# A hybrid encoder trunk: rounded value rows and sums of squares, sums given out a head pair later

## The chip, the cores and the metric

The kernel runs on one core of a Trainium2 chip, in one launch. The metric is the device time of the launch in microseconds (us), as the median of three runs. Beside it there is the trace of one profiled execution. Of the core's engines five matter here: TensorE (PE in the trace; PEld are its weight loads), VectorE (DVE), ScalarE (ACT), GpSimd (POOL) and SyncE (SP, on whose queue all DMAs are issued). Each works through its own list of instructions in order and waits for others through semaphores.

## The reference

The trunk has two layers over 16 learned tokens and 512 others, 1024 features wide. A layer is a token mixer of two parallel branches and then a gated FFN. One branch is a gated delta rule with 8 heads (GDN, solved in both directions), the other a retention with 4 heads. The output drops the learned tokens.

```python
def token_mixer(h, w_in, conv_w, ...):
    proj = h @ w_in
    (qkv_a, z_a, a_in, b_in, q_b, k_b, v_b, g_b, gate_a, gate_b) = jnp.split(proj, ...)
    qa, ka, va = jnp.split(short_conv(qkv_a, conv_w), ...)        # then l2norm of qa, ka
    g = -jnp.exp(a_log) * softplus(a_in + dt_bias);  beta = sigmoid(b_in)
    o_a = gated_delta(qa, ka, va, g, beta) forward + the same backward
    y_a = (rms(o_a) * gdn_gain * silu(z_a)) @ w_up_a
    o_b = rms(retention(qr, kr, vr) forward + backward)           # sum over m of gamma^|n-m| (q_n.k_m) v_m
    y_b = (o_b * silu(g_b)) @ w_up_b
    merged = sigmoid(gate_a) * y_a + sigmoid(gate_b) * y_b
    return merged @ w_out
for i in range(2):
    h = h + token_mixer(rms_norm(h, norm_mix[i]), ...)
    h = h + swiglu(rms_norm(h, norm_ffn[i]), ...)
return rms_norm(h, norm_final)[:, 16:]
```

`rms` needs, per token and head, a sum of squares over the head's value channels: 128 for a GDN head, 512 for a retention head.

## The kernel before, in words

Activations lie feature by token: 128 partitions of features, 528 columns of tokens (16 learned, then 4 blocks of 128). Layer 0 goes through them in two halves of 264 columns (`FULL`); layer 1, whose learned tokens are not in the output, mostly in 512 (`TAIL`).

**Projections.** A weight block of 1024 x 128 is loaded (`weights`, L183), and `split` (L177) makes two tiles in a rounded f32 type of it: the high part on ScalarE, the rest by a subtraction on VectorE. Activations are split in the same way (xh, xl). `mm3` (L193) then multiplies high by high, high by rest and rest by high: three matmuls per 128 features. Every matmul is issued by `mm`, L112, so that in the trace one tells them apart by their tiles: mmps is a projection, rpv the retention's value product, oms a sum of squares, rs the retention's scores, kvt and kvm turns of tokens, lvy, yy, oo, ks and their like the steps of a GDN head.

**The GDN heads** come in four pairs. `gdn_begin` projects the pair's q, k and v, convolves them and turns them into token rows; with the first pair `scalars` (L435) projects the 32 decay columns and turns them. `gdn_chain` then makes the products (L538), the decayed copies (L600), solves the 32-token diagonal blocks with small DMAs (L613), joins them in two levels (L629), and scans the blocks forward and backward (L723). In the levels the block matrix N is the sum of two tiles (GpSimd), small blocks are expanded to block-diagonal tiles by a product with a mask (`spread`: QT, QT2, TT on VectorE, Qf and Qb on GpSimd), and the matmuls lvy take QT, N and TT, the scan takes Qf and Qb. At the end `gdn_out` (L807) squares the head's output and its q on ScalarE, combines them on VectorE and calls `mean_square` (L790), where a plain f32 matmul with a column of ones sums over partitions. ScalarE takes the sum out of PSUM and a DMA stores it.

**Retention** (L878) has per head: two projections with rotation, scores rs with a decay strip (VectorE) and a split into prh and prl; then per 128 value channels a projection, a turn to token rows (rv, split), a gate projection, and the value product rpv: for each of the four token blocks three rounded matmuls on 128 rows, and for the 16 learned tokens one plain f32 matmul on 16 rows (prm, rvm). Squares are added up on VectorE, and `mean_square` sums them at the head's end.

**What sets the order.** `weave` (L985) runs a pair's chain and a filler side by side and gives out so much filler for so much chain; the filler is the retention heads 0 to 2 and the gates z and merge, and `retention(3)` follows the last pair. The scheduler of the framework then orders the instructions of each engine by priority and by a timeline of its own, within what buffers allow. PSUM has three pools of one bank per tile: mmps (2 buffers), the retention's and the norms' small tiles (`pt`, 2 buffers in rotation), the GDN chain's tiles (`ct`, 4 buffers). The SBUF tag "gcr" has four buffers: the pair's four broadcast decay rows, which a DMA fills from `grow`.

The work is single-file on SP: loads of weight blocks (wraw) and the small loads and stores of the chains stand in one queue in the order that the scheduler gives them.

## Time and profile before

| what | value |
|---|---|
| runs | 2978.34, 2980.01, 2978.48 us; median 2978.48 |
| profiled execution | 2975.5 us, span of the trace 2973.7 us |
| mean granted TensorE clock | 0.991 of full speed |
| TensorE | busy 2873.8 us (97%), 19519 matmuls |
| VectorE, ScalarE, GpSimd | busy 1781.4 (60%), 1038.8 (35%), 64.1 us (2%) |
| chain that ended last, by engine | TensorE 83%, VectorE 7%, DMA 6%, ScalarE 2% |

A row of the timeline gives the start (us from the span's start), the busy time of the group, the engine, the source line, the operation, output<-inputs by the program's names, partitions x elements and type, the count, and in brackets the idle time before it with what ended that. Records of matmuls overlap and their ends are modelled, so that what a matmul costs is read from one start to a later one. A plain f32 matmul leaves two records where a rounded one leaves one.

### The profile page before, as it was taken

How to read it: one execution, taken by the hardware profiler on the slowest of the kernel's cores; microseconds unless marked ns; L12 is line 12 of the kernel's file. 1: busy time of each engine (PE TensorE's matmuls, PEld its weight loads, DVE VectorE, ACT ScalarE, POOL GpSimd, SP SyncE). 2: the span in 40 equal slices, each digit the busy share in tenths (PEclk: the TensorE clock that was granted, in tenths of full speed). 3: DMA queues.
4: the chain of work that ended last, by engine and by line, in shares of the span. 5: the costliest groups of instructions: out<-in, count | busy, mean ns of one | idle time of the engine just before them, and what ended most of it. 6: DMA issues, size and time to landing. Idle time of an engine off the chain costs nothing.

```text
span 2973.7 us, 48710 instructions
## 1 busy us (share of the span) xinstructions
PE 2873.8 (97%) x19519; PEld 2578.0 (87%) x19519; DVE 1781.4 (60%) x3769; ACT 1038.8 (35%) x1967; POOL 64.1 (2%) x156
## 2 busy tenths in 40 slices
PE   8999999999999999999999999999999999999998
PEld 8998998889989998999998787887878878888887
DVE  6867867768456445333358769587685474534333
ACT  4434334244333233222244243343333332322222
POOL 0000000000000000000000000000000000000000
PEclk9999999999999999999999999999999999999999
DMA  4422323323337342333344323233234284433333
GB/s 138 111 74 75 105 75 100 84 74 107 90 106 228 118 141 81 91 93 100 115 115 115 83 76 100 71 93 97 66 101 109 74 260 126 135 99 92 98 101 99
DMA packets 506420, 313.46 MB, mean 105 GB/s; under 512 B 55632, under 2 KB 460778, under 8 KB 506194
## 3 DMA queue, kind: packets, MB, share of 16 engines
q1 hardware_dynamic: 506194, 310.35, 36.4%
q8 instruction: 153, 2.51, 0.3%
q14 instruction: 73, 0.60, 0.1%
HBM read 265.28 MB, written 45.01 MB: 104 GB/s over the span
## 4 chain that ended last, share of the span: by engine, by line
PE 83%; DVE 7%; DMA 6%; ACT 2%; issue 1%; SPq 0%; DVEq 0%; ACTq 0%
PE mmps L112 66%; PE rpv L112 3%; PE rs L112 2%; PE oo L112 2%; PE fu L112 2%; DVE wlo L118 1%; PE sn L112 1%; DMA xd<-w 1%; PE yy L112 1%; DMA gcr<-grow 1%; PE ks L112 1%; DMA lo<-od_b 1%; ACT whi L178 1%; PE oms L112 1%; PE lvy L112 1%
## 5 line engine op out<-in xcount | busy, mean ns | idle before, releaser
L112 PE MATMUL mmps<-xh,whi 128*128 128x264 f32 (+2 forms) x3888 | 1213.8, 312 | 22.8 <-ACT rp L894 9.3
L112 PE MATMUL mmps<-xh,wlo 128*128 128x264 f32 (+2 forms) x3888 | 1204.5, 310 | 1.1 <-DVE wlo L118 1.1
L112 PE MATMUL mmps<-xl,whi 128*128 128x264 f32 (+2 forms) x3888 | 1202.3, 309 | 0.0
L112 PEld LDWEIGHTS mmps<-xh,whi 128*128 128x128 f32 x3888 | 737.6, 190 | 77.6 <-issue 13.3
L112 PEld LDWEIGHTS mmps<-xh,wlo 128*128 128x128 f32 x3888 | 736.3, 189 | 44.3 <-issue 9.1
L112 PEld LDWEIGHTS mmps<-xl,whi 128*128 128x128 f32 x3888 | 736.6, 189 | 39.5 <-issue 5.9
L118 DVE TENSOR_TENSOR wlo<-wraw,whi 128x1024 fp32r<-128x1024 f32 (+1 forms) x394 | 477.3, 1212 | 486.5 <-ACT whi L178 482.0
L178 ACT CAST whi<-wraw 128x1024 fp32r<-128x1024 f32 (+1 forms) x394 | 410.0, 1041 | 936.5 <-PE mmps L112 723.7
L112 PE MATMUL mmps<-oh,whi 128*128 128x264 f32 (+2 forms) x1126 | 359.2, 320 | 3.7 <-DVE mrg L115 3.7
L112 PE MATMUL mmps<-ol,whi 128*128 128x264 f32 (+2 forms) x1126 | 358.6, 319 | 0.0
L112 PE MATMUL mmps<-oh,wlo 128*128 128x264 f32 (+2 forms) x1126 | 357.9, 318 | 0.0
L112 PEld LDWEIGHTS mmps<-oh,whi 128*128 128x128 f32 x1126 | 211.7, 188 | 21.6 <-ACT oh L178 3.4
L112 PEld LDWEIGHTS mmps<-ol,whi 128*128 128x128 f32 x1126 | 211.7, 188 | 16.5 <-issue 1.3
L112 PEld LDWEIGHTS mmps<-oh,wlo 128*128 128x128 f32 x1126 | 211.9, 188 | 15.6
L115 DVE SCALAR_TENSOR_TENSOR ac<-xc,cw,ac 128x528 f32<-128x528 f32 x192 | 146.7, 764 | 8.1 <-ACT ac L125 1.7
L118 DVE TENSOR_TENSOR ff<-fg,mmps 128x264 f32<-128x264 f32 (+1 forms) x63 | 32.5, 516 | 116.8 <-PE mmps L112 116.8
L112 PE MATMUL rpv<-prh,rv 128*128 128x264 f32 (+1 forms) x384 | 98.4, 328 | 0.0
L118 DVE TENSOR_TENSOR st<-w 68x30 f32<-68x30 f32 (+14 forms) x240 | 78.3, 326 | 28.1 <-DMA w<-ndm 16.4
L125 ACT ACTIVATE gth<-mmps 128x264 f32<-128x264 f32 (+1 forms) x135 | 61.3, 454 | 68.3 <-PE mmps L112 67.9
L118 DVE TENSOR_TENSOR w<-w,st 68x30 f32<-68x30 f32 (+14 forms) x240 | 78.0, 325 | 6.0
L112 PE MATMUL rs<-rot 128*128 128x264 f32 (+3 forms) x240 | 77.9, 456 | 0.7 <-DVE pr L118 0.7
L112 PEld LDWEIGHTS rpv<-prh,rv 128*128 128x128 f32 x384 | 65.3, 188 | 10.5 <-issue 6.0
(298 smaller groups left out, 3064.6 us busy)
## 6 DMA issues: line engine op xcount, KB each, us to landing
wraw<-in_w_in_dram SPq DMA_DIRECT2D x194, 512.0 KB
wraw<-in_w_ffn_in_dram SPq DMA_DIRECT2D x88, 512.0 KB
wraw<-in_w_up_b_dram SPq DMA_DIRECT2D x32, 512.0 KB
wraw<-in_w_ffn_out_dram SPq DMA_DIRECT2D x32, 512.0 KB
gcr<-grow SPq DMA_DIRECT2D x32, 264.0 KB
wraw<-in_w_up_a_dram SPq DMA_DIRECT2D x16, 512.0 KB
wraw<-in_w_out_dram SPq DMA_DIRECT2D x16, 512.0 KB
wraw<-in_w_ffn_out_dram SPq DMA_DIRECT2D x16, 384.0 KB
```

Source lines behind the costliest of these rows:

```text
L112: newest[0] = nc.tensor.matmul(o, lhsT=l, rhs=r, start=start, stop=stop)
L115: (eng or nc.vector).scalar_tensor_tensor(out=o, in0=a, scalar=s, in1=b, op0=op0, op1=op1)
L118: (eng or nc.vector).tensor_tensor(out=o, in0=a, in1=b, op=op)
L125: nc.scalar.activation(o, a, f, **kw)
L178: nc.scalar.copy(hi, src)
```

## The change

Five things are changed.

1. The value product's learned tokens: scores and values of the 16 learned tokens are split too and laid under one another in tiles of 96 rows (pst: high, rest, high; vst: high, high, rest; 16 rows used of each 32), so that one rounded matmul sums the three products.
2. The sums of squares: the summed tile is split (osh, osl for GDN heads; prh, prl for retention heads), and two rounded matmuls with a rounded column of ones take the place of one f32 matmul.
3. A pair's or head's sums are put on a list (`later`) and issued afterwards by `sums`: in the next pair's `gdn_begin` after its second head's front and at its end, in the next retention head behind its rotation, and at the end of the mixing. The square of a GDN head's q moves from `gdn_out` to the decayed copies. osh and osl take buffers of the tag "gcr".
4. The decay columns: high part and rest of the 32 columns' weights lie side by side in one tile, so that two matmuls per 128 features do; the two halves of the result are added after the turns, which are 64 columns wide.
5. In the levels N is added on VectorE, and Qf and Qb are expanded on ScalarE, four activations each, with the mask's column as the scale.

```diff
+    one = cp.tile([P, 1], F32R, name="one")
+    nc.scalar.copy(one, ones[:, 0:1])
...
     def scalars():
+
         ab = gp.tile([P, L], F32, name="ab", tag="gcr", bufs=4)
-
-        def consume(t, n0, n, ps):
-            nc.vector.tensor_copy(ab[0:32, n0:n0 + n], ps[0:32])
-        project(W, C_AB, 1, xn, FULL, consume)
+        with tc.high_priority(offset=lead[0]):
+            raw = wp.tile([P, 8, P], F32, name="wraw", tag="wraw", bufs=WB[0])
+            nc.sync.dma_start(raw, W[:, C_AB:C_AB + P].rearrange("(k p) c -> p k c", p=P))
+            w = wp.tile([P, 8, P], F32R, name="whi", tag="whi", bufs=WB[1])
+            nc.scalar.copy(w, raw)
+            tt(w[:, :, 32:64], raw[:, :, 0:32], w[:, :, 0:32].bitcast(F32), SUB)
+        for n0, n in FULL:
+            ps = pmm.tile([P, 512], F32, name="mmps", tag="mm")
+            for k in range(KT):
+                for j, t in enumerate(xn):
+                    mm(ps[:, :n], w[:, k, :], t[k][:, n0:n0 + n], start=k + j == 0, stop=k + j == KT)
+            nc.vector.tensor_copy(ab[0:64, n0:n0 + n], ps[0:64, :n])
         ps = ct("abt")
         for c in range(NC):
-            nc.tensor.transpose(ps[:, c * 32:(c + 1) * 32], ab[0:32, NM + c * P:NM + (c + 1) * P], ident[:32, :32])
-        nc.tensor.transpose(ps[0:NM, P:P + 32], ab[0:32, 0:NM], ident[:32, :32])
+            nc.tensor.transpose(ps[:, c * 64:(c + 1) * 64], ab[0:64, NM + c * P:NM + (c + 1) * P], ident[:64, :64])
+        nc.tensor.transpose(ps[0:NM, 256:320], ab[0:64, 0:NM], ident[:64, :64])
         abt = gp.tile([P, NCH, 2, 16], F32, name="abt", tag="sc", bufs=SB)
         nc.vector.memset(abt[:, NC], 0.0)
-        nc.vector.tensor_copy(abt[:, 0:NC].rearrange("p c s h -> p (c s h)"), ps[:, 0:P])
-        nc.vector.tensor_copy(abt[0:NM, NC].rearrange("p s h -> p (s h)"), ps[0:NM, P:P + 32])
+        for n, c0, c1 in ((P, 0, NC), (NM, NC, NCH)):
+            o = abt[0:n, c0:c1].rearrange("p c s h -> p c (s h)")
+            a = ps[0:n, c0 * 64:c1 * 64].rearrange("p (c j e) -> p c j e", j=2, e=32)
+            nc.vector.tensor_copy(o, a[:, :, 0])
+            tt(o, o, a[:, :, 1], ADD)
...
@@ -604,6 +618,7 @@
             gr = s["gr"][d]
             act(gr, gr, AF.Exp)
             tt(gr, gr, s["q"], MUL)
+        act(s["q"][:, t0:L], s["q"][:, t0:L], AF.Square)
         for c in range(NCH):
             n = tok(c)[1]
...
@@ -634,7 +649,7 @@
         xd = st["xd"]
         nn, nb = s["N"]
         fl = lambda a: a.rearrange("p c d -> p (c d)")
-        tt(fl(nn), fl(nn), fl(nb), ADD, eng=nc.gpsimd)
+        tt(fl(nn), fl(nn), fl(nb), ADD)
...
-        def spread(o, a, m, n, eng=None):
+        def spread(o, a, m, n):
             tt(o.rearrange("p c (b i) -> p c b i", b=n), bc(a.unsqueeze(2), [P, NC, n, 32]),
-               bc(m.unsqueeze(1).unsqueeze(3), [P, NC, n, 32]), MUL, eng=eng)
+               bc(m.unsqueeze(1).unsqueeze(3), [P, NC, n, 32]), MUL)
...
         T, Q, Qf, Qb = (gp.tile([P, NC, P], F32, name=n, tag="NQ", bufs=8) for n in ("QT", "QT2", "Qf", "Qb"))
         TT = gp.tile([P, NC, 64], F32, name="TT", tag="sc", bufs=SB)
         spread(T, tm, cst["bm"], 4)
         spread(Q, qm, cst["bm"], 4)
         spread(TT, tl, cst["bm2"], 2)
-        spread(Qf, qf, cst["bm"], 4, nc.gpsimd)
-        spread(Qb, qb, cst["bm"], 4, nc.gpsimd)
+        for o, a in ((Qf, qf), (Qb, qb)):
+            for b in range(4):
+                act(o[:, :, b * 32:b * 32 + 32], a, AF.Copy, scale=cst["bm"][:, b:b + 1])
...
@@ -792,7 +808,8 @@
         ms = ms[0:1]
         for n0, n in tail:
             ps = pt("oms")
-            mm(ps[0:1, :n], ones[:, 0:1], sq[:, n0:n0 + n])
+            for j in range(2):
+                mm(ps[0:1, :n], one, sq[j][:, n0:n0 + n], start=j == 0, stop=j == 1)
             act(ms[:, n0:n0 + n], ps[0:1, :n], AF.Copy, scale=scale, bias=bias)
         nc.sync.dma_start(msd[row:row + 1, :], ms[:, t0:L])
...
-    def gdn_out(h, st):
+    def gdn_squares(h, st):
+
         s = st[h]
         (o, om), q = s["o"], s["q"]
         o = o.rearrange("p c d -> p (c d)")
@@ -814,11 +832,18 @@
         if not last:
             nc.sync.dma_start(od_a[h, :, 0:NM], om)
             act(sq[:, 0:NM], om, AF.Square)
-        act(q[:, t0:L], q[:, t0:L], AF.Square)
         stt(sq[:, t0:L], q[:, t0:L], 128.0 * 128.0 * EPS, sq[:, t0:L], MUL, ADD)
+        hi, lo = (gp.tile([P, L], F32R, name=n, tag="gcr", bufs=4) for n in ("osh", "osl"))
+        split(hi[:, t0:L], lo[:, t0:L], sq[:, t0:L])
+        later.append(lambda ps: mean_square(h, (hi, lo), 4.0 / 128.0, 4 * 128 * EPS * 4 * EPS, tmp("ms"), ps))
         yield 1.0
-        mean_square(h, sq, 4.0 / 128.0, 4 * 128 * EPS * 4 * EPS, s["gr"][0], ct)
-        yield 1.0
+
+    later = []
+
+    def sums(ps):
+
+        while later:
+            later.pop(0)(ps)
...
+                if h == hs[1]:
+                    sums(ct)
                 lead[0] = PRI
...
         for _ in sc:
             pass
+        sums(ct)
...
-        for pair in zip(*[gdn_out(h, st) for h in hs]):
-            yield sum(pair)
+        for h in hs:
+            yield from gdn_squares(h, st)
+
+
+
+    pst = rp.tile([96, L], F32R, name="pst")
+    vsts = [rp.tile([96, P], F32R, name=f"vst{q}") for q in range(2)]
+    for t in (pst, *vsts):
+        nc.gpsimd.memset(t.bitcast(F32), 0.0)
...
         q, k = rot
+        sums(pt)
         yield from filler
         pr = []
         for c in range(NCH):
             m0, m = tok(c)
-            o = tmp("pr") if c < NC else rp.tile([P, L], F32, name="prm", tag="prm")
+            o = tmp("pr")
...
                 pr.append((hi, lo))
             else:
-                pr.append(o)
+                split(pst[0:NM, t0:L], pst[32:32 + NM, t0:L], o[0:NM, t0:L])
+                nc.scalar.copy(pst[64:64 + NM, t0:L], pst[0:NM, t0:L].bitcast(F32))
             yield 1.8
...
             rv = rp.tile([P, 2, NC * P], F32R, name="rv", tag="rot", bufs=2)
             vh, vl = rv[:, 0], rv[:, 1]
-            vm = rp.tile([NM, P], F32, name="rvm", tag="rvm", bufs=2)
+            vst = vsts[dv % 2]
             ps = pt("rvt")
             for c in range(NC):
                 n0, n = tok(c)
@@ -942,7 +979,8 @@
             split(vh, vl, ps)
             pm = pt("rvm")
             nc.tensor.transpose(pm[0:NM, 0:P], vc[:, 0:NM], ident)
-            nc.scalar.copy(vm, pm[0:NM, 0:P])
+            split(vst[0:NM], vst[64:64 + NM], pm[0:NM, 0:P])
+            nc.scalar.copy(vst[32:32 + NM], vst[0:NM].bitcast(F32))
             gs = tmp("rg")
...
                 for c in range(NC):
                     for a, b in ((vh, 0), (vh, 1), (vl, 0)):
                         mm(ps[:, :n], a[:, c * P:(c + 1) * P], pr[c][b][:, n0:n0 + n], start=c + b == 0 and a is vh, stop=False)
-                mm(ps[:, :n], vm, pr[NC][0:NM, n0:n0 + n], start=False)
+                mm(ps[:, :n], vst, pst[:, n0:n0 + n], start=False)
...
             nc.sync.dma_start(od_b[h * 4 + dv, :, t0:L], o[:, t0:L])
             if dv:
                 tt(sqa[:, t0:L], sqa[:, t0:L], sq[:, t0:L], ADD)
             yield 4.5
-        mean_square(H + h, sqa, 4.0 / DV, 4 * 256 * EPS, tmp("ms"), pt)
+        sq = [rp.tile([P, L], F32R, name=n, tag=n, bufs=4) for n in ("prh", "prl")]
+        split(sq[0][:, t0:L], sq[1][:, t0:L], sqa[:, t0:L])
+        later.append(lambda ps: mean_square(H + h, sq, 4.0 / DV, 4 * 256 * EPS, tmp("ms"), ps))
...
     for _ in retention(3, merge_gates(14, 16)):
         pass
+    sums(pt)
     mixctx.close()
```

The framework's scheduler orders the result anew. Two places show it, both on TensorE in layer 1. The first is the end of a pair's scan, between the third and the fourth pair. yy and oo are the scan's last matmuls, oms the sums of squares, kvt and kvm the turns of the next pair's tokens, mmps projections. Before:

```order
L112 MATMUL yy<-r,Qf 128x128 x2
L112 MATMUL oo<-gcr,S 128x128 x2
L112 MATMUL oo<-P,xx 128x128 x2
L112 MATMUL oms<-qk,c_ones 1x512 x2
L525 MATMUL kvt<-c_ident,qk 128x128 x4
L526 MATMUL kvm<-c_ident,qk 16x128
L526 MATMUL kvm<-c_ident,v_23772 16x128
L525 MATMUL kvt<-c_ident,v_23772 128x128 x4
L112 MATMUL mmps<-xh,whi 128x264
```

The same place of the changed kernel:

```order
L112 MATMUL yy<-r,Qf 128x128 x2
L112 MATMUL oo<-gcr,S 128x128 x2
L112 MATMUL oo<-P,xx 128x128
L539 MATMUL kvt<-c_ident,qk 128x128 x4
L112 MATMUL oo<-P,xx 128x128
L540 MATMUL kvm<-c_ident,qk 16x128
L540 MATMUL kvm<-c_ident,v_24000 16x128
L539 MATMUL kvt<-c_ident,v_24000 128x128 x4
L112 MATMUL mmps<-xh,whi 128x264
```

The sums are gone from between the scan and the turns. They stand 24 projection matmuls later, one at a time, the last of the four 19 projection matmuls behind the first. At layer 0's pair ends the order is the same in kind, with the first sums about 35 projection matmuls behind the turns.

The second place is the last pair of layer 1, at the end of its scan. rpv are the value products of the fourth retention head, rs its scores. Before, the scan's matmuls stand among that head's:

```order
L112 MATMUL rpv<-prh,rv 128x512
L112 MATMUL oo<-P,xx 128x128
L112 MATMUL rpv<-prh,rv 128x512
L112 MATMUL oo<-P,xx 128x128
L112 MATMUL rpv<-prl,rv 128x512
L112 MATMUL rpv<-prh,rv 128x512 x2
```

In the changed kernel:

```order
L112 MATMUL ks<-S,qk 128x128 x2
L112 MATMUL yy<-r,Qf 128x128 x2
L112 MATMUL oo<-gcr,S 128x128 x2
L112 MATMUL oo<-P,xx 128x128 x2
L112 MATMUL oms<-osh,one 1x512 x2
L112 MATMUL oms<-osl,one 1x512 x2
L112 MATMUL rs<-rot 128x512 x4
L112 MATMUL mmps<-xh,whi 128x264
```

Before, that head's projections, scores and value products lay between the scan's steps, and the pair's two sums came between projections (`mmps<-xl,whi`, `oms<-qk,c_ones` x2, `mmps<-xh,wlo`). Now the head's q and k projections stand earlier, the scan's steps follow one another, and the sums stand straight behind the scan and ahead of the head's scores. At the end of layer 0's last pair the order is the same: eight oo, eight oms, then rs.

## Rows read from the trace of the kernel before

**Rows 1.** The page: busy time of each engine (share of the span) xinstructions.
```profile
PE 2873.8 (97%) x19519; PEld 2578.0 (87%) x19519; DVE 1781.4 (60%) x3769; ACT 1038.8 (35%) x1967; POOL 64.1 (2%) x156
```
**Rows 2.** Waits of TensorE: waiting tile <- releaser; us in all, count, the longest.
```profile
PE lvy L112 <- DVE QT L118: 13.8, 8, 4.9
```
**Rows 3.** Chain that ended last, in order of time: start, us, engine, tile, xcount.
```profile
40.01 22.73 PE mmps L112 x186
...
2609.49 249.62 PE mmps L112 x1078
```
**Rows 4.** Timeline of TensorE, a value product in layer 0: start, busy, instruction.
```profile
297.04 0.29 PE L112 MATMUL rpv<-prh,rv 128*128 128x264 f32 x1
297.26 0.71 PE L112 MATMUL rpv<-prm,rvm 16*128 16x264 f32 x2
...
298.13 0.28 PE L112 MATMUL rpv<-prl,rv 128*128 128x264 f32 x1
```
**Rows 5.** The same timeline, a value product in layer 1.
```profile
1861.14 0.40 PE L112 MATMUL rpv<-prh,rv 128*128 128x512 f32 x1
1861.47 1.12 PE L112 MATMUL rpv<-prm,rvm 16*128 16x512 f32 x2
...
1862.75 0.28 PE L112 MATMUL mmps<-xl,whi 128*128 128x264 f32 x1
```
**Rows 6.** The same, a retention head's two sums in layer 0.
```profile
304.16 0.28 PE L112 MATMUL mmps<-xh,wlo 128*128 128x264 f32 x1
304.38 1.05 PE L112 MATMUL oms<-rsq,c_ones 128*1 128x264 f32 x4
...
305.58 0.28 PE L112 MATMUL mmps<-xl,whi 128*128 128x264 f32 x1
```
**Rows 7.** The same, the end of a pair in layer 0; idle time before in brackets.
```profile
451.10 0.39 PE L112 MATMUL oo<-Pm,xx 16*128 16x16 f32 x2
452.04 1.05 PE L112 MATMUL oms<-qk,c_ones 128*1 128x264 f32 x4 [0.55 <-DVE qk L115]
...
457.30 0.39 PE L112 MATMUL mmps<-xh,whi 128*128 128x264 f32 x1 [0.45 <-ACT xc L507]
```
**Rows 8.** Groups by form: operation xcount | busy us, mean ns | idle before, releaser.
```profile
L178 ACT CAST prh<-pr 128x528 fp32r<-128x528 f32 x16 | 10.2, 635 | 33.5 <-DVE pr L118 30.6 <-DVE Nm L567 2.8
L118 DVE TENSOR_TENSOR prl<-pr,prh 128x528 fp32r<-128x528 f32 x16 | 11.3, 703 | 3.2 <-ACT prh L178 3.1
```
**Rows 9.** Timeline of TensorE and ScalarE, the end of a pair in layer 1.
```profile
2136.13 0.49 PE L112 MATMUL yy<-r,Qf 128*128 128x128 f32 x2 [1.18 <-DVE r L115]
2136.90 0.65 PE L112 MATMUL oo<-P,xx 128*128 128x128 f32 x4
2137.78 1.15 ACT L125 ACTIVATE qk<-o 128x512 f32<-128x512 f32 x2
2139.19 3.43 PE L112 MATMUL oms<-qk,c_ones 128*1 128x512 f32 x4 [1.64 <-DVE qk L115]
...
2144.91 0.39 PE L112 MATMUL mmps<-xh,whi 128*128 128x264 f32 x1 [0.96 <-ACT xc L507]
```
**Rows 10.** Window, length, busy (xcount) of PE, PEld, DVE, ACT, POOL; PEclk, DMA, GB/s.
```profile
2140.00:2150.00 10.00, 9.04 (x55) 6.34 (x53) 5.41 (x10) 4.68 (x9) 0.13 (x2) 0.86 0.29 56
```
**Rows 11.** Timeline of GpSimd, VectorE and TensorE in the levels, layer 1.
```profile
1700.55 1.04 POOL L118 TENSOR_TENSOR Qb<-qe,c_bm 128x512 f32<-128x512 f32 x1 [5.08 <-DVE qe L651]
1700.94 0.93 DVE L118 TENSOR_TENSOR TT<-qe,c_bm 128x256 f32<-128x256 f32 x1
1701.79 1.28 DVE L118 TENSOR_TENSOR QT<-qd,c_bm 128x512 f32<-128x512 f32 x2
1702.61 2.05 PE L112 MATMUL lvy<-QT,N 128*128 128x128 f32 x8 [4.01 <-DVE QT L118]
```
**Rows 12.** Timeline of the queue of SyncE, layer 0: start, us of the group, issue.
```profile
266.74 1.15 SPq L554 DMA_DIRECT2D gcr<-grow  x2
275.96 21.91 SPq L187 DMA_DIRECT2D wraw<-in_w_in_dram  x4
```

More of the change, by code (lines that the diff above doesn't have):

```diff
@@ L382, in layer @@
 def layer(tc, nc, env, l, xn, gd):
-    (x, meta, newest, lead, cp, dp, wp, xp, tp, mm, stt, tt, ts, act, tmp, ctmp, pt, ct, pmm, cst, ident, ones, cw, gain,
+    (x, meta, newest, lead, cp, dp, wp, xp, tp, mm, stt, tt, ts, act, tmp, ctmp, pt, ct, pmm, cst, ident, ones, one, cw, gain,
      prm, softplus, inverse_root, nea, lg, lgn, hd, split, weights, mm3, FULL, TAIL, Norm, xtiles,
@@ L386, in layer @@
         "x", "meta", "newest", "lead", "cp", "dp", "wp", "xp", "tp", "mm", "stt", "tt", "ts", "act", "tmp", "ctmp", "pt", "ct", "pmm",
-        "cst", "ident", "ones", "cw", "gain", "prm", "softplus", "inverse_root", "nea", "lg", "lgn",
+        "cst", "ident", "ones", "one", "cw", "gain", "prm", "softplus", "inverse_root", "nea", "lg", "lgn",
         "hd", "split", "weights", "mm3", "FULL", "TAIL", "Norm", "xtiles", "first_units",
```

## Prediction

> **What bounds the kernel now.** I read the engines' busy shares first. TensorE is busy 97% of the span, VectorE 60%, ScalarE 35%, GpSimd 2% [rows 1]. The reader is to see that an instruction taken off VectorE, ScalarE or GpSimd is worth nothing by itself. What counts is TensorE's own time and the few places where TensorE stands still. Second, the waits: the longest of those that the change touches is TensorE's for a block table in the levels, 13.8 us in all [rows 2]. Third, the chain that ended last. It is TensorE for 83%, in stretches that hold nothing but projection matmuls, and these give the price of one pass of the rounded type: 22.73/186 = 0.122 us for 264 columns in layer 0, 249.62/1078 = 0.232 us for 512 columns in layer 1 [rows 3]. Last, TensorE's timeline at the lines that the diff touches. Records there overlap, so a cost is read from start to start, less the passes between.
>
> **The change, part by part**, against the profiled execution (2975.5 us; its span is 2973.7).
>
> A. *Learned tokens' value rows.* In layer 0 a 16-row f32 matmul stands between rounded ones. From the start of the one before it to the start of the second one behind it are 298.13 - 297.04 = 1.09 us; without the two passes of 0.122 it takes 0.846 [rows 4]. In layer 1 the same reading gives 1862.75 - 1861.14 = 1.61, less 0.232 and 0.122, that is 1.256 [rows 5]. After the change one rounded matmul on 96 rows stands there, one pass. No row shows a rounded matmul on 96 rows; the f32 one on 16 rows costs more than four rounded passes on 128, so fewer rows give no rebate and I take a full pass, 0.122 and 0.232, with nothing below it and the f32 price above. There are 4 heads x 4 column blocks x 2 halves = 32 in layer 0, and 16 in layer 1: 32 x 0.724 + 16 x 1.024 = 23.2 + 16.4 = **39.6 us**. All of it is TensorE's own time with work behind it.
>
> The four passes of an f32 matmul alone would be 4 x 0.122 = 0.489 and 4 x 0.232 = 0.926; the rows show 0.36 and 0.33 us more. The Trainium skill ("FP8 and Floating Point Precision", TensorE Precision Notes) says that true FP32 runs as four passes and names nothing further. By that rule alone A would be 32 x 0.367 + 16 x 0.694 = 22.8 us; the trace shows the larger sum, and the first rival asks whether the rest goes too.
>
> B. *Decay columns.* The projection runs 2 matmuls per row block and half where it ran 3: 32 fewer of 264 columns, 32 x 0.122 = **3.9 us**. Its transposes double in width and stay four and one.
>
> C. *Retention's sums of squares.* In layer 0 two f32 matmuls onto one row take 305.58 - 304.16 = 1.42 less two passes, 1.18 us [rows 6]; four rounded ones take 0.49. Four heads: 2.8. Layer 1 has one f32 of 512 columns per head; it is priced as in rows 5, 1.256 against 0.46, four heads: 3.2. Together **6.0 us**.
>
> D. *The pair ends.* Behind a pair's scan TensorE waits for squares, sums them, and only then turns the next heads' tokens. In layer 0 projections resume at 457.30, 6.2 us after the scan's last matmul at 451.10 [rows 7]. After the change the turns come straight behind the scan and the sums some 40 matmuls later. What holds the projection then is the older squares' chain on ScalarE (square, two splits, conv), which I place at 455.1: a splitting pass costs 0.64 on ScalarE and 0.70 on VectorE for 528 columns [rows 8]. Saved 2.2, less 4 x 0.122 for the later sums, 1.7, three times: 5.1. In layer 1 the scan's last matmul stands at 2136.90, the squares at 2137.78, and two f32 sums take 3.43 where eight passes of 0.232 would be 1.85, so that projections resume at 2144.91 [rows 9]. Without the sums: 2137.78 + 2 x 0.57 for the squares + 0.59 + 0.59 + 0.38 for the evictions = 2140.6. Saved 4.3, less 4 x 0.232, 3.4, three times: 10.2. Sum **15.3 us**. Below it is bounded by 0 (something else holds TensorE to the same moment), above by the full gaps, 3 x 6.2 + 3 x 8.0 = 43.
>
> E. *The last pair of each layer.* This goes the other way. Before, the fourth retention head's scores and value rows lay between that pair's scan steps and the sums stood among projections. Now the order puts the sums ahead of that head's scores, since both draw the same PSUM tiles: the scan runs bare, and TensorE then waits for square, product and both splits with nothing to fill. I take a bare scan at about 1.3, square 0.6, product 0.7, splits 0.64 + 0.70, the second head's splits and the evictions about 2, near 6.0 to 6.5 per layer, since the clock falls over such gaps (0.86 on the mean in the 10 us from 2140, after TensorE had waited, so partly 1.2 instead of 2.4 GHz [rows 10]). The sums' own f32 time goes, 1.5 per layer. Net -12.5 + 3.0 = **-9.5 us**; the ends are -22 (each wait as long as two of the layer-1 pair ends' gaps) and 0.
>
> F. *The levels.* The sum N moves to VectorE, which is what TensorE waits for: 16 times about 0.64 on the path, unless hidden. Qb's expansion leaves GpSimd; it runs beside VectorE's TT, which takes 0.93 us at 256 columns where QT takes 0.64 at 512 [rows 11]. So about 0.5 comes back. The ScalarE expansions (eight per head, 0.16 to 0.64 each) are needed two steps later. I take **0**, with ends of -10 (all 16 additions) and +14 (all of rows 2).
>
> The Trainium skill ("SBUF — State Buffer", Who interferes with whom) has the same rule: a VectorE operation with two SBUF inputs and a GpSimd one that reads SBUF hold each other up. The slow TT agrees; by that rule F would be +5 to +8 us and the time some 6 us less.
>
> G. *Added casts, subtractions and copies* (201 instructions more on ScalarE, 84 on VectorE). TensorE's 97% hides them where they are not in E: VectorE and ScalarE stand idle 40% and 65% of the span. If the cover were gone, 24 splits of the sums at 1.34 would be 32 us, the worst that the range knows. On SP's queue the next pair's four gcr loads now wait for the sums, because osh and osl take the same four buffers, and weight loads stand behind them. Before, the gcr loads go out at 266.74 and the weights at 275.96, for use later still [rows 12]; some 42 matmuls, 5.5 us, fit into that gap. Cost 0.
>
> Sum: 39.6 + 3.9 + 6.0 + 15.3 - 9.5 + 0 = 55.3, so 2975.5 - 55.3 = 2920.2 for a profiled execution. The median of the runs, 2978.48, stands 3.0 above the profiled one, so I forecast **2923 us**.
>
> **The rivals.**
>
> 1. *Only the passes come back.* The 0.36 and 0.33 us in A beyond the passes, and the same in C, may belong to the change of tile shape or weights, which remains. For it: a weight load of another row count stands there after as before. Against it: the two f32 records themselves fill 0.71 and 1.12 us of it [rows 4, 5]. A is then 22.8 and C 4 x 0.49 + 4 x 0.46 = 3.8, 19 us less: 2942.
>
> 2. *VectorE becomes the bound in the levels and scans.* N's sums, the subtractions and the products all stand on one in-order engine that TensorE waits for there, and the scans have lost filler where f32 value rows stood. For it: rows 2. Against it: its 60%. F at its lower end, -10, and E at -22 cost 22 us more: 2946.
>
> 3. *The pair ends keep their length*, since the next projection waits for ScalarE's conv either way [rows 7]. D is 0: 2938.
>
> 4. *Slower than before*: the gcr loads hold SP's queue. One mechanism: they wait for TensorE's sums, which now stand behind the next pair's projections, and those need weights that queue behind the gcr loads. With some 8 us of slack in rows 12 it costs nothing until the sums come 8 us later than the old ones; beyond, each us is lost six times. To eat 55 us it would need 17 us after the resumption, three times the 5.5 counted. The time would be about 2985.
>
> **How the numbers follow.** Chances: the forecast 0.62, rival 1 0.12, rival 2 0.14, rival 3 0.09, rival 4 0.03. The forecast's own range is 2907 to 2937: E's waits halved and F at +10 below, half of D and E's waits half as long again above. The range of 8 in 10 goes below to E at 0 with F near its upper end, above past rivals 1 to 3 by half of one of them: 2902 to 2956. This measurement cannot tell less than 0.2%, about 6 us. The forecast and rivals 1 to 3 clear it, 0.97; I move 0.03 of that to no change, for several of them at once. Faster 0.94, same 0.03, slower 0.03.
>
> **What would show it.** Right: value rows of one kind only, 0.122 and 0.232 start to start through the learned tokens' matmul (A); projection restarts some 4 us behind the scan in layer 0 and 5 in layer 1, with sums among projections (D); a new wait of 4 to 7 us before the fourth head's scores, ended by VectorE's split (E); the wait for QT no longer than 13.8 us in all (F). Wrong: a value-row matmul on 96 rows that takes more than a pass; weight matmuls that wait for a DMA after the pair ends; a wait before the scores beyond 10 us.

## The result, and the profile after

The changed kernel takes 2956.4 us in the median of four runs (2954.66 to 2963.42), the kernel before in runs beside them 2978.89. The ratio is 0.9926 (95% interval 0.9911 to 0.9942): 22 us faster where 55 were forecast. The time lies 0.4 us above the range.

The page's head, in the form of [rows 1], with the span ahead of it:

```profile
span 2961.6 us, 48741 instructions
PE 2835.6 (96%) x19439; PEld 2580.0 (87%) x19439; DVE 1802.2 (61%) x3853; ACT 1100.8 (37%) x2168; POOL 8.9 (0%) x114
```

TensorE's busy time fell from 2873.8 to 2835.6, by 38 us. But span less busy time, which is TensorE's idle time, was 2973.7 - 2873.8 = 99.9 us and is now 126.0. So 26 us of what came off TensorE came back as waiting. Two things blur this pair of profiles. The profiled execution of the changed kernel is the slowest of its four (2963.42 us), so that the spans differ by 12 us and the medians by 22. And its granted clock is 0.986 where that of before is 0.991: (0.991 - 0.986) x 2973.7, some 15 us of TensorE's busy time. By this estimate some 53 us of work came off, not 38.

The work itself came off as the rows of before said. TensorE's timeline at a value product, layer 0 and then layer 1 (start, busy, instruction), answers to [rows 4, 5]:

```profile
159.18 0.28 PE L112 MATMUL rpv<-prh,rv 128*128 128x264 f32 x1
159.30 0.29 PE L112 MATMUL rpv<-pst,vst 96*128 96x264 f32 x1
159.42 0.29 PE L112 MATMUL rpv<-prh,rv 128*128 128x264 f32 x1
...
1652.48 0.40 PE L112 MATMUL rpv<-prh,rv 128*128 128x512 f32 x1
1652.71 0.40 PE L112 MATMUL rpv<-pst,vst 96*128 96x512 f32 x1
1652.95 0.29 PE L112 MATMUL mmps<-xh,wlo 128*128 128x264 f32 x1
```

From 159.30 to 159.42 is one pass of 0.12 us, and from 1652.71 to 1652.95 one of 0.24. Nothing beyond a pass is left.

The end of a pair, layer 0 and layer 1, answers to [rows 7, 9]:

```profile
446.40 0.39 PE L112 MATMUL oo<-Pm,xx 16*128 16x16 f32 x2
446.72 0.66 PE L539 MATMUL kvt<-c_ident,qk 128*128 128x128 f32 x4
...
448.58 0.40 PE L112 MATMUL oms<-osh,one 128*1 128x264 f32 x2 [0.55 <-ACT osh L178]
...
449.63 0.28 PE L112 MATMUL mmps<-xh,whi 128*128 128x264 f32 x1
...
2125.16 0.39 PE L112 MATMUL oo<-P,xx 128*128 128x128 f32 x2
2125.39 0.60 PE L539 MATMUL kvt<-c_ident,qk 128*128 128x128 f32 x4
...
2128.35 0.39 PE L112 MATMUL mmps<-xh,whi 128*128 128x264 f32 x1 [1.49 <-ACT xc L521]
```

In layer 0 projections resume 3.2 us after the scan's last matmul where it was 6.2. The first head's sums still stand ahead of them there, with waits of TensorE for its splits (0.55 us before the row shown). In layer 1, from the first of the scan's last two products as in [rows 9], it is 2128.35 - 2125.16 = 3.2 us where it was 8.0. That 8.0 was not typical: the other two pair ends of layer 1 took 6.2 us before (1753.71 to 1759.94 and 1947.16 to 1953.39).

The last pair of layer 0, TensorE:

```profile
820.90 0.39 PE L112 MATMUL oo<-Pm,xx 16*128 16x16 f32 x2
822.56 0.43 PE L112 MATMUL oms<-osh,one 128*1 128x264 f32 x2 [1.27 <-ACT osh L178]
823.30 0.60 PE L112 MATMUL oms<-osl,one 128*1 128x264 f32 x2 [0.31 <-DVE osl L118]
824.94 0.60 PE L112 MATMUL oms<-osh,one 128*1 128x264 f32 x2 [1.04 <-ACT osh L178]
...
826.53 2.13 PE L112 MATMUL rs<-rot 128*128 128x264 f32 x4 [0.25 <-ACT ms L125]
...
842.53 1.43 PE L112 MATMUL rs<-rot 128*128 128x264 f32 x4 [3.05 <-DVE pr L118]
```

and VectorE just before that last row:

```profile
841.36 0.77 DVE L115 SCALAR_TENSOR_TENSOR lo<-lo,gain,rs 128x528 f32<-128x528 f32 x1 [8.00 <-DMA lo<-od_a]
842.04 0.42 DVE L118 TENSOR_TENSOR pr<-rs,strip 128x264 f32<-128x264 f32 x1
```

The scores start 5.6 us after the bare scan. Then they wait again: VectorE has stood 8.0 us on a load of the next stage (lo, from od_a), with the scores' eviction pr behind it in its list. The windows over this place show what follows the waits (the number before the DMA share is the granted clock):

```profile
820.00:830.00 10.00, 6.99 (x31) 4.54 (x31) 3.27 (x8) 4.47 (x12) 0.00 (x0) 0.66 0.23 82
830.00:840.00 10.00, 9.48 (x72) 9.00 (x70) 2.29 (x11) 1.73 (x3) 0.00 (x0) 1.00 0.29 58
840.00:850.00 10.00, 7.47 (x38) 6.83 (x38) 7.53 (x13) 3.31 (x5) 0.00 (x0) 0.83 0.92 310
```

Waits of TensorE (us in all, times, longest), answering to [rows 2]; the ones shown for the retention heads grew:

```profile
PE mmps L112 <- ACT rp L929: 11.8, 6, 4.6
PE rs L112 <- DVE pr L118: 11.0, 8, 3.0
...
PE lvy L112 <- DVE QT L118: 10.0, 6, 2.9
...
PE rvt L978 <- ACT rvc L970: 5.5, 5, 2.1
PE mmps L112 <- DVE rg L115: 4.7, 3, 2.6
```

The same four waits of the kernel before:

```profile
PE mmps L112 <- ACT rp L894: 9.3, 6, 2.4
...
PE rvt L941 <- ACT rvc L933: 3.2, 4, 1.7
...
PE mmps L112 <- DVE rg L115: 3.1, 4, 1.6
...
PE rs L112 <- DVE pr L118: 0.7, 1, 0.7
```

The wait for QT is shorter (13.8 before). The waits for evictions of the retention heads (rp, pr, rvc, rg) are 33 us together, and were 16. Most of the new idle time is there.

### The profile page after: what moved, and what is told of

Same layout as the page of the kernel before. It is cut to its first block, busy times and chain, and to the rows that moved or that the text cites. A ratio compares the mean times of both kernels' runs of the same rounds, so it can differ in the third digit from the quotient of the medians.

```text
span 2961.6 us, 48741 instructions
## 1 busy us (share of the span) xinstructions
PE 2835.6 (96%) x19439; PEld 2580.0 (87%) x19439; DVE 1802.2 (61%) x3853; ACT 1100.8 (37%) x2168; POOL 8.9 (0%) x114
## 4 chain that ended last, share of the span: by engine, by line
PE 80%; DVE 8%; DMA 7%; ACT 2%; issue 1%; SPq 0%; DVEq 0%; ACTq 0%
PE mmps L112 65%; PE rpv L112 3%; PE oo L112 2%; PE fu L112 1%; DVE wlo L118 1%; PE rs L112 1%; PE sn L112 1%; PE yy L112 1%; DMA lo<-od_b 1%; DMA xd<-w 1%; PE ks L112 1%; DMA lo<-od_a 1%; ACT whi L178 1%; DVE N L115 1%; DMA wraw<-in_w_in_dram 1%
## 5 line engine op out<-in xcount | busy, mean ns | idle before, releaser
L112 PE MATMUL mmps<-xh,wlo 128*128 128x264 f32 (+1 forms) x3856 | 1197.4, 311 | 0.8 <-DVE wlo L118 0.8
L112 PEld LDWEIGHTS rs<-rot 128*128 128x128 f32 (+1 forms) x240 | 38.6, 175 | 38.8 <-DVE pr L118 14.6
```

The lines of the kernel that those rows point to most:

```text
L112: newest[0] = nc.tensor.matmul(o, lhsT=l, rhs=r, start=start, stop=stop)
```

## The experiments

Five executions or more were timed for most kernels, beside runs of the kernel before on the same chip. In the table, us is (ratio - 1) x 2985, the median of before on these chips; idle is span less TensorE's busy time in the one profiled execution (99.9 for the kernel before, 126.0 for the changed one); clock is (1 - mean granted clock) x time over the timed executions, the time given up at the lower level, half of the time spent there (39 to 41 for the kernel before, 42 for the changed one). The profiled executions lie up to 7 us from the medians of their kernels, so a difference of a few us in idle time means little.

| run | what | ratio (95%) | us | idle | clock |
|---|---|---|---|---|---|
| after | the whole change | 0.9926 (0.9911-0.9942) | -22 | 126.0 | 42 |
| e3 | before + rounded value rows | 0.9970 (0.9958-0.9981) | -9 | 124.2 | 48 |
| e8 | after, value rows f32 | 0.9978 (0.9969-0.9987) | -7 | 107.1 | 37 |
| e11 | before + value rows, high parts only | 0.9973 (0.9963-0.9982) | -8 | 113.8 | 42 |
| e12 | before + splits that nothing reads | 1.0029 (1.0017-1.0040) | +9 | 114.3 | 40 |
| e5 | e3 + 38 us of zero passes | 1.0055 (1.0042-1.0069) | +16 | 117.6 | 44 |
| e16 | before + 38 us of zero passes | 1.0129 (1.0116-1.0142) | +39 | 104.5 | 37 |
| e4 | after, sums at once | 1.0116 (1.0097-1.0134) | +35 | 148.2 | 89 |
| e6 | e4 + f32 sums in the wait | 1.0104 (1.0087-1.0120) | +31 | 136.4 | 78 |
| e7 | after, sums f32, late | 0.9889 (0.9876-0.9903) | -33 | 108.9 | 35 |
| e1 | after, last sums behind scores | 0.9916 (0.9903-0.9930) | -25 | 123.1 | 45 |
| e2 | after, levels on GpSimd | 0.9925 (0.9913-0.9937) | -22 | 126.1 | 43 |
| e9 | before, weave 88 | 1.0032 (1.0020-1.0043) | +10 | 105.5 | 45 |
| e10 | before + one 128x1 copy | 1.0015 (1.0006-1.0023) | +4 | 104.3 | 42 |
| e13 | e3, weave 88 | 0.9959 (0.9947-0.9972) | -12 | 120.4 | 44 |
| e14 | e3, weave 80 | 0.9987 (0.9977-0.9998) | -4 | 129.1 | 44 |
| e15 | e7, weave 80 | 0.9937 (0.9926-0.9949) | -19 | 118.1 | 35 |
| e17 | after, weave 88 | 0.9879 (0.9862-0.9897) | -36 | 115.6 | 32 |
| e18 | e7 + e1 | 0.9890 (0.9872-0.9907) | -33 | 103.7 | 38 |

**First round: which part lost it.** e1, the last pair's sums behind the fourth head's scores:

```diff
-        sums(pt)
+        if h < 3:
+            sums(pt)
...
+        if h == 3:
+            sums(pt)
         sqa = rp.tile([P, SW], F32, name="rsq", tag="strip")[:, 0:L]
```

> The changed kernel, with one edit: the fourth retention head gives out the last pair's sums behind its scores instead of ahead of them. Theory 1 (in the changed kernel the early sums make the next stage's inverse roots and its od_a products ready early, and these stand with their DMA waits on VectorE's in-order queue between the fourth head's scores): the waits of TensorE on pr and on evictions between the last scan and the first matmul on oh go from about 11 and 8 us to under 3 each, with the lowered clock behind them; 15 to 25 us off, 2932 to 2941 us. Theory 2 (the f32 matmuls were cover for chains on VectorE and ScalarE all along the kernel, so their passes came back only in part): that stretch is a small part, under 6 us off, 2950 to 2957. Theory 3 (the additions on VectorE and expansions on ScalarE in the levels): no difference, 2953 to 2960.

3 us faster than the changed kernel, and the intervals overlap. The stretch from layer 0's last pair to the next stage lost some of its waits; other stretches gained some. Theory 1 falls as the main cause.

e2, the levels' addition and expansions back on GpSimd:

```diff
-        tt(fl(nn), fl(nn), fl(nb), ADD)
+        tt(fl(nn), fl(nn), fl(nb), ADD, eng=nc.gpsimd)
...
-        for o, a in ((Qf, qf), (Qb, qb)):
-            for b in range(4):
-                act(o[:, :, b * 32:b * 32 + 32], a, AF.Copy, scale=cst["bm"][:, b:b + 1])
+        spread(Qf, qf, cst["bm"], 4, nc.gpsimd)
+        spread(Qb, qb, cst["bm"], 4, nc.gpsimd)
```

> The changed kernel with its fifth part undone: N is added and Qf and Qb are expanded on GpSimd again. Theory 1: within 5 us of the changed kernel, 2951 to 2961 us. Theory 2: the same within 5 us. Theory 3 (VectorE is what TensorE waits for, and N's addition lengthens it): at least 8 us faster than the changed kernel, below 2948. If the levels gained by the move: TensorE's wait for QT is back at some 14 us, and the time some 4 us longer, 2960.

The same time. Its waits for QT are 20.5 us where the changed kernel has 10.0, and others are shorter. The move in the levels is worth nothing measurable in time, though VectorE did gain by it. The view of tile TT (least/median/greatest ns), before and after:

```profile
L118 DVE TENSOR_TENSOR TT<-qe,c_bm x16: 404/928/940, 191.1 to 2262.5; 128x256 f32<-128x256 f32 x16
```

```profile
L118 DVE TENSOR_TENSOR TT<-qe,c_bm x16: 413/425/427, 192.3 to 2250.3; 128x256 f32<-128x256 f32 x16
```

With the expansion back on GpSimd, in e2, the median is 928 ns again.

e3, the first part of the change alone on the kernel before:

```diff
...
-                pr.append(o)
+                split(pst[0:NM, t0:L], pst[32:32 + NM, t0:L], o[0:NM, t0:L])
+                nc.scalar.copy(pst[64:64 + NM, t0:L], pst[0:NM, t0:L].bitcast(F32))
...
-            nc.scalar.copy(vm, pm[0:NM, 0:P])
+            split(vst[0:NM], vst[64:64 + NM], pm[0:NM, 0:P])
+            nc.scalar.copy(vst[32:32 + NM], vst[0:NM].bitcast(F32))
...
-                mm(ps[:, :n], vm, pr[NC][0:NM, n0:n0 + n], start=False)
+                mm(ps[:, :n], vst, pst[:, n0:n0 + n], start=False)
```

> The kernel before with the first part alone: value rows of the learned tokens in the rounded type. Theory 1: the full 39.6 us come back, 2936 to 2942 us, since the sums and the last pair's order are as before. Theory 2: half of it or less, 2955 to 2965, with TensorE's idle time up by 10 us or more against the kernel before, on waits for VectorE and ScalarE within the first three pairs.

9 us come back of 39.6. In this order, most of the loss is here. e4, the deferral undone:

```diff
         for h in hs:
             yield from gdn_squares(h, st)
+        sums(ct)
...
-        later.append(lambda ps: mean_square(H + h, sq, 4.0 / DV, 4 * 256 * EPS, tmp("ms"), ps))
+        mean_square(H + h, sq, 4.0 / DV, 4 * 256 * EPS, tmp("ms"), pt)
```

> The changed kernel with its third part undone: sums in the rounded type, but given out at a pair's end and at a retention head's end, as before. Forecast of part D: 15 us come back at the six pair ends only by the deferral, so this one is that much slower there; the next stage's inverse roots stand as early at the last pair as in the changed kernel, so its gaps there stay (theory 1): 2965 to 2972 us. Theory 2: deferral is worth little, 2954 to 2962.

57 us slower than the changed kernel, far more than forecast: 22 us more idle time and 47 us more given up at the lower clock. In this order, rounded sums given out at once are dear.

**Second round: work, clock or order.** e5 puts passes back behind the rounded value rows:

```diff
+    zst = rp.tile([96, P], F32R, name="zst")
...
-                mm(ps[:, :n], vst, pst[:, n0:n0 + n], start=False)
+                mm(ps[:, :n], vst, pst[:, n0:n0 + n], start=False, stop=False)
+                nb = 4 if last else 6
+                for b in range(nb):
+                    mm(ps[:, :n], zst, pst[:, n0:n0 + n], start=False, stop=b == nb - 1)
```

> The kernel before with the first part alone (value rows rounded, as in the run before), and behind each such matmul rounded passes with zero weights, six in layer 0 and four in layer 1, which put back 32 x 6 x 0.122 + 16 x 4 x 0.232 = 38 us of TensorE work and change nothing else. Cover theory (those passes stood where other engines or the clock set the end): the time is that of the rounded value rows alone within 12 us, ratio to the kernel before 0.997 to 1.001, with TensorE's idle time and its time at the lower clock back near those of the kernel before (94 and 51 us against 116 and 102). Order theory (the scheduler's new order is unlucky and the work itself was on the path): the passes cost what they take, ratio 1.008 to 1.013.

The time lies between the two theories. 38 us of passes cost 25 us (1.0055 against 0.9970), and idle time fell by only 7 us. With TensorE's work as before, this kernel is 16 us slower than the kernel before.

e6 fills the wait of e4 with f32 sums of the unsquared outputs, into the bank that the real sums overwrite:

```diff
+            if o is not None:
+                mm(ps[0:1, :264], ones[:, 0:1], o[:, 0:264])
+                if last:
+                    mm(ps[0:1, :248], ones[:, 0:1], o[:, 264:512])
             for j in range(2):
```

> The changed kernel with its third part undone (sums at the pair's end) and one thing added: while the squares and splits run, TensorE sums the unsquared head outputs in plain f32 into the same PSUM bank, which the real sums overwrite; 16 heads, some 1.2 us of work each, 19 us in all. Clock theory (the 180 us at the lower clock are what makes that kernel slow, and TensorE falls to it where it waits): time at the lower clock falls by 50 us or more, and the time falls by 15 to 35 us, ratio to the kernel before 1.000 to 1.007, although TensorE has more to do. If idle time alone counts: the waits stay as long, and the time is the same or longer, ratio 1.010 to 1.016.

The time given up at the lower clock fell by 11 us against e4, so the time spent at it by some 21, not by 50; the time fell by 4, with overlapping intervals. 19 us more work cost nothing, but it kept the clock up only in small part. Inconclusive.

e7, the GDN heads' sums in f32 and given out late, without splits; the retention heads' sums are f32 at the head's end, as before:

```diff
-            for j in range(2):
-                mm(ps[0:1, :n], one, sq[j][:, n0:n0 + n], start=j == 0, stop=j == 1)
+            mm(ps[0:1, :n], ones[:, 0:1], sq[:, n0:n0 + n])
...
-        split(hi[:, t0:L], lo[:, t0:L], sq[:, t0:L])
+        so = gp.tile([P, L], F32, name="oso", tag="gcr", bufs=4)
+        stt(so[:, t0:L], q[:, t0:L], 128.0 * 128.0 * EPS, sq[:, t0:L], MUL, ADD)
...
+        mean_square(H + h, sqa, 4.0 / DV, 4 * 256 * EPS, tmp("ms"), pt)
```

> The changed kernel with its second part undone and its third kept: a GDN head's sum is one plain f32 matmul again, given out late as in the changed kernel, from a tile of its own; no splits. The retention heads' sums are f32 at the head's end, as before. Cover theory: TensorE has 16 us more work at places with projections before and behind it, and VectorE and ScalarE lose 32 and more splitting passes of some 0.65 us; the time is within 8 us of the changed kernel's, ratio 0.990 to 0.995. If the sums' passes are what pays: ratio 0.997 or more.

11 us faster than the changed kernel, just past the better end of what was expected: rounding the sums was no gain in this order. e8, the changed kernel with f32 value rows, the edit of e3 the other way round:

```diff
-                mm(ps[:, :n], vst, pst[:, n0:n0 + n], start=False)
+                mm(ps[:, :n], vm, pr[NC][0:NM, n0:n0 + n], start=False)
```

> The changed kernel with its first part undone: the learned tokens' value rows are plain f32 matmuls on 16 rows again, 39.6 us more TensorE work by the rows of before. Cover theory: between 5 and 18 us of it shows, ratio to the kernel before 0.994 to 0.999. Work on the path: all of it shows, the ratio is 1.004 to 1.008. If the deferral did all and the value rows nothing: ratio 0.991 to 0.994.

The first part is worth 0.9978 - 0.9926, 15 us, within the changed kernel.

**Third round: the splits, or the order.** e9 changes one number of the kernel before:

```diff
-NB = 86.0
+NB = 88.0
```

> The kernel before with one number changed, the filler's share in the weave of chain and filler from 86 to 88: no instruction is added or removed, only the order moves (nearly all of TensorE's and VectorE's lists). Order theory (the kernel before stands in an order that its numbers were fitted to, and any edit that makes the scheduler order anew loses 10 to 30 us of that, whatever the work): slower by 5 to 30 us, ratio 1.002 to 1.010, with more idle time and more time at the lower clock than 94 and 51 us. If order is worth little: ratio 0.998 to 1.002.

9.5 us slower with the same instructions. e10:

```diff
-    nea = cp.tile([P, 32], F32, name="nea")
+    one = cp.tile([P, 1], F32R, name="one"); nc.scalar.copy(one, ones[:, 0:1]); nea = cp.tile([P, 32], F32, name="nea")
```

> The kernel before with one operation more at the start, a ScalarE copy of a 128x1 column that nothing reads; the work is the same, and parts of the lists of VectorE, ScalarE and the DMA queue are ordered anew. Order theory: ratio 1.000 to 1.008, more often above 1.002 than not. If order is worth little: ratio 0.998 to 1.002.

4 us slower. e11, high parts only:

```diff
...
+                prm = rp.tile([NM, L], F32R, name="prm", tag="prm")
+                nc.scalar.copy(prm[:, t0:L], o[0:NM, t0:L])
+                pr.append(prm)
...
-            vm = rp.tile([NM, P], F32, name="rvm", tag="rvm", bufs=2)
+            vm = rp.tile([NM, P], F32R, name="rvm", tag="rvm", bufs=2)
```

> The kernel before with the learned tokens' value rows in the rounded type, but the high parts alone (the products with the rests are left out): one pass in place of the f32 matmul, and hardly an operation more on VectorE and ScalarE. Splits theory (the splits and copies of the first part hold up ScalarE, VectorE and the small PSUM tiles): all of the 39.6 us come back, ratio 0.985 to 0.989. Order theory: as with all three products, ratio 0.992 to 1.000.

As fast as e3 without its splits. But it is no fair comparison, since a rounded matmul on 16 rows does not take one pass (last section): by the trace e11 takes 32 x (0.846 - 0.51) + 16 x (1.256 - 0.62), some 21 us of work off and not 39.6, and 8 us come back. That neither bears the splits theory out nor rules it out. e12, on the kernel before, makes the split of the values (not that of the scores):

```diff
+    vsts = [rp.tile([96, P], F32R, name=f"vst{q}") for q in range(1)]
...
             nc.scalar.copy(vm, pm[0:NM, 0:P])
+            vst = vsts[0]
+            split(vst[0:NM], vst[64:64 + NM], pm[0:NM, 0:P])
+            nc.scalar.copy(vst[32:32 + NM], vst[0:NM].bitcast(F32))
```

> The kernel before with the split and the copy of the learned tokens' value rows made as in the changed kernel (16 times per layer, two operations on ScalarE and one on VectorE), and read by nothing: the value product stays f32. Splits theory: slower by 12 us or more, ratio 1.004 or above, with TensorE's idle time up. Order theory: anything between 1.000 and 1.010. If neither: 0.998 to 1.002.

9 us slower, no more than e9 with no instruction added. The three kernels that keep the f32 value rows and differ in order or in small operations all lie 4 to 10 us above the kernel before, so its order is probably a favourable one.

**Fourth round: the same edits in other orders.** e13 and e14 are e3 with the weave's share at 88 and 80. The line in e13, and then in e14:

```diff
-NB = 86.0
+NB = 88.0
```

```diff
-NB = 86.0
+NB = 80.0
```

> Rounded value rows on the kernel before, with the weave's share at 88; the kernel before with 88 was at ratio 1.0032. Cover theory: TensorE's waits eat a third to a half of the 39.6 us under any order: 16 to 27 us below the kernel before at 88, ratio 0.994 to 0.998. Order theory (the removed work counts in full once both stand in orders fitted to neither): 35 us or more below it, ratio 0.989 to 0.992.

> The same with the weave's share at 80. Order theory: the times of the rounded value rows spread by 10 us or more over the shares, and one of 80 and 88 is clearly below the 0.997 at 86. Cover theory: all three within 5 us, ratio 0.995 to 0.999.

Between e9 and e13, which share the number 88, the value rows are worth 0.0073, 22 us, as the cover theory had it; e14 lies 8 us above e13, between what the two theories allowed. e15 is e7 at 80, the same line:

> The fastest kernel so far (rounded value rows, f32 sums given out late, ratio 0.9889) with the weave's share at 80. Order theory: it moves by up to 10 us either way, 0.985 to 0.993. Cover theory: within 4 us, 0.9875 to 0.9903.

14 us slower than at 86, worse than I allowed: one number moves the same work by that much. e16 is the kernel before with the zero passes in front of the f32 matmul:

```diff
+    zst = rp.tile([P, P], F32R, name="zst")
...
+                nb = 4 if last else 6
+                for b in range(nb):
+                    mm(ps[:, :n], zst, pr[0][0][:, n0:n0 + n], start=False, stop=False)
                 mm(ps[:, :n], vm, pr[NC][0:NM, n0:n0 + n], start=False)
```

> The kernel before, value rows in f32 as they were, plus 38 us of rounded zero-weight passes in the same products (six in layer 0, four in layer 1). If TensorE is the bound there at the margin: 34 to 45 us slower, ratio 1.0115 to 1.015. If its passes stand half under waits of others: 15 to 27 us slower, ratio 1.005 to 1.009.

The full price, 38.5 us: work added to the kernel before counts one for one, where the same passes added to e3 counted for 25 us (e5). e17 is the changed kernel with `NB = 88.0`:

> The changed kernel with the weave's share at 88 and nothing else. If order is a spread of some 10 us around the same work: ratio 0.989 to 0.996. If the changed kernel stands in an unlucky order: 0.988 or less. Either way TensorE's idle time stays above 110 us, as in every kernel so far with rounded value rows but the one with f32 sums.

0.9879, 36 us faster than the kernel before at its own share of 86, and 46 us faster than the kernel before at 88. Idle time is 115.6 us in the table's measure, above the 110 of the expectation, where e9 has 105.5; the waits that its trace names add up to 107. It beats both kernels: 2947.33 us against 2983.47 for the kernel before on that chip. Pages of e9 and of e17:

```profile
span 2995.4 us, 48690 instructions
PE 2889.9 (96%) x19519; PEld 2582.7 (86%) x19519; DVE 1785.8 (60%) x3769; ACT 1037.2 (35%) x1967; POOL 71.7 (2%) x156
```

```profile
span 2942.9 us, 48764 instructions
PE 2827.3 (96%) x19439; PEld 2571.2 (87%) x19439; DVE 1801.0 (61%) x3853; ACT 1101.5 (37%) x2168; POOL 8.9 (0%) x114
```

At the same share TensorE's busy time falls by 63 us and its idle time rises by 10; at 86 it was 38 and 26. The busy times hold a part that is the clock's: the profiled executions had 0.985 (e9) and 0.990 (e17), 0.991 and 0.986 at 86. Some 15 us are to be taken off the 63 and added to the 38, so that by this estimate about as much work came off at either share, 48 and 53 us. What differs is the waiting, and the time given up at the lower clock, which falls by 13 us from e9 to e17 and hardly moves at 86. The four waits of the retention heads grew here too, from 14 us in e9 to 28. e18 joins the edits of e7 and e1:

> Rounded value rows, f32 sums given out late, and the last pair's sums behind the fourth head's scores. From the parts (0.9889, and 3 us for the place of the last sums): ratio 0.987 to 0.990, 2946 to 2955 us. If the place of the last sums is only order: 0.985 to 0.993.

As e7 alone; the place of the last sums is worth nothing measurable beside late f32 sums.

## Why the prediction was wrong

**Failed: step A's sentence that all of it is TensorE's own time with work behind it.** The size of the work was right: one pass stands where 0.846 and 1.256 us stood. What it is worth was not. The value rows against f32, three times with everything else alike:

| pair | work | more idle | more clock loss | left | timed |
|---|---|---|---|---|---|
| before, share 86 (e3) | 39.6 | 24.3 | 7.1 | 8 | 9 |
| before, share 88 (e9, e13) | 39.6 | 14.9 | -1.8 | 26 | 22 |
| changed, share 86 (e8, after) | 39.6 | 18.9 | 5.0 | 16 | 15 |

The account closes within 5 us each time, with idle from one execution: 15 to 24 us of the 39.6 turn into waits of TensorE, and the clock takes up to 7 more. A busy share of 97% said that TensorE's work counts one for one. Added to the kernel before it does (e16, 38.5 us for 38); added to e3 it counts for two thirds (e5, 25 us for 38); taken off it counted for a quarter to just over a half.

**Failed with it: no term for the order.** The sum took it that nothing changes but the costs. The scheduler orders everything anew, and of the two shares that both kernels were given, 86 suits the kernel before and 88 the changed one: 88 makes the first 9.5 us slower and the second 14 us faster. That is 24 of the 33 us between 55 and 22. Against e9 the change is worth 46 us. One other share was tried on the changed kernel, so part of this may be luck; at 80 e7 lost 14 us (e15).

**What stays open.** Whether the new waits in A come from lost cover or from the new order and operations is not separated. Putting passes back (e5) removed only 7 us of idle time; unread splits (e12) added 14, one unread copy (e10) 4, both in new orders too. e11, with fewer operations, came back with 8 of some 21 us, which settles nothing either. No order was held fixed while work was taken out.

Point by point for the rest. **B** was not run by itself. **C**: the sums' passes came off, but e7 with f32 sums is faster at 86, so the 6 us are not shown as a gain; e7 also gives the retention heads' sums out at once, which is not tried by itself. **D** was right in size, 16 us for 15.3, but in part by luck. The six pair ends are 3.3, 3.0, 3.1 and 3.0, 3.0, 4.8 us shorter, 20.3 in all, less 3 x 0.5 and 3 x 0.9 for the later sums: 7.9 in layer 0 for 5.1, and 8.1 in layer 1 for 10.2. The forecast had tripled the one pair end of layer 1 whose f32 sums ran slowly (3.43 us [rows 9]; the other two resumed 1.8 us sooner); its sum for the resumption there comes to 2140.5 and not 2140.6, which changes nothing. Without deferral, the rounded sums made the changed kernel 57 us slower (e4). **E** was right in place and nearly in size: 5.6 us in layer 0, and 2308.96 - 2303.93 = 5.0 in layer 1, for 6.0 to 6.5; most of the waits ended with ScalarE's split, not VectorE's. I did not see the second wait behind it, VectorE's 8.0 us on the next stage's load; in e1, where the load no longer stands ahead of the scores' evictions, the time is 3 us less, with intervals that overlap. **F** at 0 was right (e2): TT did get faster without GpSimd beside it, 0.43 us for 0.93, but no time came of it. **G**: TensorE's wait for weights (whi) is 0.5 us in all in both kernels, so no wait of TensorE shows SP's queue; unread splits cost 9 us, within what order costs.

The rivals. The first falls by its own rows: nothing beyond a pass is left. What stood beyond the passes did belong to the shape, as it said, but to that of 16 rows (last section), and went with it. The second named a time (2946) and idle time on VectorE's and ScalarE's evictions that came nearest, but put it in the levels, where the wait became shorter; it was in the retention heads. The third and fourth fall with the pair ends' rows.

## What to carry to other kernels

In a kernel whose order a scheduler makes, work taken off the busiest engine need not be worth its time: measure the slope both ways, and compare kernel with kernel over several settings of the number that paces them, since one setting moved the same work by 3 to 14 us here. Read the clock of two profiles before comparing their busy times. An edit that turns one matmul into split, split and two cheap matmuls puts two more operations in front of them: given out at once they made the changed kernel 57 us slower than given out late (e4), and given out late they still were no gain over f32 (e7). After such a change fit the pacing number again before judging it: the change was worth 22 us at the old one and 36 at another.

## What the runs showed of the hardware

A rounded matmul on 16 rows between matmuls on 128 rows is dear by its shape alone. In e11, TensorE:

```profile
151.00 0.28 PE L112 MATMUL rpv<-prh,rv 128*128 128x264 f32 x1
151.22 0.38 PE L112 MATMUL rpv<-prm,rvm 16*128 16x264 f32 x1
151.53 0.39 PE L112 MATMUL rpv<-prh,rv 128*128 128x264 f32 x1
151.75 0.28 PE L112 MATMUL rpv<-prl,rv 128*128 128x264 f32 x1
```

Read as in [rows 4], from 151.00 to 151.75 are 0.75 us, less two passes 0.51, where one pass is 0.122; on 96 rows, in the first rows of the section on the result, it takes the 0.12. In layer 1 it is 1655.62 - 1654.65 = 0.97, less 0.232 and 0.122, 0.62 for a pass of 0.232. So the rounded matmul on 16 rows takes 0.39 us more than its pass in either layer, and the f32 one took 0.36 and 0.33 more than its four: what stood there beyond the passes goes with the 16 rows and not with the type.

A second surprise was how much of e4 is the clock: its mean granted clock over the timed executions is 0.9705, where the kernel before has 0.9864 in the runs beside it, and its windows show the lower level while TensorE is busy throughout, behind a window with waits:

```profile
400.00:410.00 10.00, 7.53 (x49) 6.74 (x49) 3.57 (x9) 2.70 (x9) 0.00 (x0) 0.66 0.01 2
410.00:420.00 10.00, 10.00 (x52) 8.69 (x53) 5.65 (x18) 3.53 (x12) 0.00 (x0) 0.66 0.00 0
```

A mean of 0.66 is a mix of 2.4 and 1.2 GHz, mostly the lower.
